# A hybrid decoder trunk step: tokens in two halves, or in five groups with two head pairs in flight

## The chip, the cores and the metric

The kernel runs on one core of one Trainium2 chip. The metric is the device time of one execution in microseconds (us), lower is better. The engines are TensorE (PE; its weight loads are shown apart as PEld), VectorE (DVE), ScalarE (ACT), GpSimd (POOL) and SyncE (SP, which only issues transfers here). Each takes its instructions in the order in which the compiled program has them. The framework in which the kernel is written chooses that order when the program is built, from a model of the durations, with the program text as priority; nothing is reordered between engines while it runs, so a wait for a late result holds up everything behind it on the same engine.

## The reference, cut to what matters

```python
D_MODEL = 1024; SEQ = 2048; DEC_BATCH = 8; DEC_SEQ = 8      # 2048 prompt tokens, 64 sample tokens
CONV_W = RWKV_W = 512; HEAD_DIM = 64; N_HEADS_RWKV = 8
IN_COLS = 4*512 + 4*512 + 64 + 64                            # 4224 = 33 tiles of 128 columns
...
xn = rms_norm(x, norm_g)
p = xn @ w_in                                                # 1024 -> 4224
u = cg * h; z = causal 3-tap conv over u; y_conv = bg * z * silu(gc)
pr = pr + mu_shift * (pr_prev - pr)                          # token shift: r, k, v, wl, al, gr
decay = exp(-DECAY_SCALE * sigmoid(w0 + tanh(wl) @ w_dec2)); a = sigmoid(a0 + al @ w_a2)
kk = normalised k * k_k
S_t = S_{t-1} diag(w_t) + (S_{t-1} (-kk_t)) (kk_t*a_t)^T + v_t k_t^T ;  o_t = S_t r_t     # per head, 64 x 64
y_rwkv = (group_norm(o) + bonus) * silu(gr)
x + concat[y_conv, y_rwkv] @ w_out, then a final rms_norm
```

Everything is float32. The prompt starts from a zero state, each of the 8 samples of 8 tokens from its own state.

## The kernel before, in words

**Layout.** Features lie on the 128 partitions and tokens along the free axis. Each large product is written as three: operands are split into a high part (rounded to the engine's faster float32 form) and a low remainder, and `project` (L305) adds high x high, high x low and low x high: 24 products for one 128-column tile of weights and one block of tokens, into one PSUM bank `pj` (two of them).

**Tokens.** The prompt is cut into two halves of 1024 (`half_blocks`, L79), each into blocks of 256, 384 and 384 tokens; the 64 sample tokens ride with the first block of the first half (330 columns with the shifted predecessors). `xprep` (L209) normalises, transposes and splits the tokens of a whole half.

**Weights.** `load_w` (L290) loads a 512 KB tile of `w_in` in the first half, splits it on ACT and POOL, and stores both parts (1 MB) to DRAM; in the second half both parts are loaded by POOL's DMA queue, into two buffers each.

**Stages.** The main loop (L923) takes 8 steps, one for each half and pair of heads. A step has: `rwkv_pair` (L423), four weight tiles (k, r, v, gate) over three blocks, each block followed by the decays, the mask products `amat` (L534; PSUM tile `ax`, 128 x 128 of scores for each 64-token chunk and head), and the rest; `inverse` (L633), which inverts the triangular 64 x 64 matrix of each chunk: the 32 x 32 diagonal blocks go through DRAM (`dn`, then `na`), are solved by a substitution of 31 steps with two DVE instructions each (`subst`, L607; tiles `sub` and `xi`), return through DRAM (`dx`, then `AB`), and two rounds of small products fill in the off-diagonal block; `wkv` (L719), the chain over the 16 chunks of 64 tokens, one after the other; and `conv_group` (L325), four weight tiles of the convolution branch, which depend on nothing of the chain. Because the order is chosen by modelled time, the conv products are placed into the gaps of `inverse` and `wkv`.

**One chunk** (`chunk`, L722) works on two heads of 64 channels, in quarters of the PE array: `ca<-sv,L` and `oo<-sv,L` (state and values against both score matrices), `cb<-sv,bt`; a DVE copy `xs`; `ca<-xs,AB`; a DVE scaling `u`; `cb<-u,bt` and `oo<-u,AB`; and one DVE instruction for each head that writes the next state. These are 12 products, or 24 instructions, since one in plain float32 is two passes.

**Output.** After all 8 steps `out_weights` (L876) loads and splits `w_out`, and `out_tile` (L890) runs 17 times over 128 tokens: 48 products of 512 columns with tokens on the partitions, residual, norm and store.

Of the kernel before, what the change touches and what calls it, by code (L numbers as in the profile page):

```python
# [17 lines left out]
D = 1024  # L18
# [8 lines left out]
HALF = SEQ // 2  # L27
CONV_COLS = 4 * CW
DS = math.exp(-0.5)
# [3 lines left out]
TW = 386  # L33

C_ID, C_BONES, C_HSEL = 0, 128, 256
NCONST = 258
C_MASK, C_SMASK, C_SCM, C_SCS, C_BM = 0, 128, 256, 640, 704
NMASK = 712

P_MU, P_KK, P_KA, P_RK, P_LG, P_LB, P_W0, P_A0, P_CW = 0, 17, 21, 25, 29, 33, 37, 41, 45  # L40
NPRM = 57


def constants():
# [7 lines left out]
    c[:, C_ID:C_ID + 128] = p[:, None] == p[None, :]  # L52
    strict = (s[:, None] < t[None, :])
    incl = (s[:, None] <= t[None, :])
    same = (s[:, None] // 8 == t[None, :] // 8)
    m[:, C_MASK:C_MASK + 64] = strict
    m[:, C_MASK + 64:C_MASK + 128] = incl
    m[:, C_SMASK:C_SMASK + 64] = strict & same
    m[:, C_SMASK + 64:C_SMASK + 128] = incl & same
    c[:, C_BONES:C_BONES + 128] = (p[:, None] // 64) == (p[None, :] // 64)  # L60
    c[:, C_HSEL] = p < 64
    c[:, C_HSEL + 1] = p >= 64
    m[:, C_SCM:C_SCM + 384] = (np.arange(384) % 64 != 0)[None, :]
# [5 lines left out]
class Blk:  # L69
    def __init__(self, i, cols, c0, np_, p0, samp, base):  # L70
        self.i, self.cols, self.c0, self.np, self.p0, self.samp = i, cols, c0, np_, p0, samp
        self.o = base + p0
        self.t0 = 0 if samp else self.o
        self.nt = np_ + (SAMP if samp else 0)
        self.ch0 = p0 // CH
        self.nch = np_ // CH


def half_blocks(hf):  # L79
    if hf == 0:  # L80
        return [Blk(0, 330, 74, 256, 0, True, SAMP), Blk(1, 384, 0, 384, 256, False, SAMP),
                Blk(2, 384, 0, 384, 640, False, SAMP)]
    return [Blk(0, 256, 0, 256, 0, False, 0), Blk(1, 384, 0, 384, 256, False, 0),
            Blk(2, 384, 0, 384, 640, False, 0)]
# [3 lines left out]
def trunk_kernel(ctx, tc, I, O):  # L88
# [4 lines left out]
    for nm in ("const", "xn", "w", "half", "pair", "tmp", "small", "ch"):  # L93
        pools[nm] = ctx.enter_context(tc.tile_pool(name=nm, bufs=1))
# [4 lines left out]
    def T(pool, shape, tag, bufs=1, dt=F32):  # L99
        cnt[0] += 1  # L100
        return pools[pool].tile(shape, dt, tag=tag, bufs=bufs, name=f"{tag}_{cnt[0]}")

# [10 lines left out]
    def tmp():  # L113
        return T("tmp", [128, TW], "t", 7)

# [11 lines left out]

    def mm(out, lhsT, rhs, start=True, stop=True):
        pe.matmul(out, lhsT=lhsT, rhs=rhs, start=start, stop=stop)  # L129

    yd = [[dram.tile([D, bl.nt], F32, name=f"yd{hf}{bl.i}") for bl in half_blocks(hf)] for hf in range(2)]
# [7 lines left out]
    bones = cst[:, C_BONES:C_BONES + 128]  # L139
    hsel = cst[:, C_HSEL:C_HSEL + 2]  # L140
    msk = T("const", [128, NMASK], "msk", 1, BF16)
    bmask = msk[:, C_BM:C_BM + 8]

    def rowtile():
        return T("half", [128, HALF + SAMP], "la0", 1)[:, :D]


# [40 lines left out]
    def rsqrt(x, n, rows=128, tag="x"):  # L188

        w = {"g": 6, "n": 3, "x": 1}[tag]  # L190
        nb = 2
        y = T("small", [128, w], "nwy" + tag, nb)[:rows, :n]
        a = T("small", [128, w], "nwa" + tag, nb)[:rows, :n]
# [10 lines left out]

# [4 lines left out]
    def xprep(hf):  # L209
        grow = rowtile()  # L210
        if hf == 1:
            act.dma_start(out=grow, in_=I["norm_g"].partition_broadcast(128).rearrange("p a d -> p (a d)"))
        if hf == 0:
            act.dma_start(out=cst[:, 0:128], in_=I["consts"][:, 0:128])
        xh, xl = [], []
        stage = [0]

        def staging():
            stage[0] += 1
# [6 lines left out]
        for bl in half_blocks(hf):  # L226
# [11 lines left out]
            if bl.samp:  # L238
                pool.memset(ss, 1.0)
# [779 lines left out]
```

## Time and profile before

| | |
|---|---|
| median of 3 runs | 1636.35 us (1623.49 to 1639.68) |
| the profiled execution: its time / its span in the trace | 1631.2 us / 1629.4 us |
| mean granted TensorE clock | 0.966 of 2.4 GHz |
| instructions | 29,336, of them 11,088 matmuls |
| PE / DVE / ACT / POOL busy | 93% / 62% / 38% / 18% |
| bytes moved | 151.9 MB |

The profile gives each instruction's start and length. Matmuls are pipelined, so their lengths overlap: what a product costs is the distance from its start to the next one's. "pj<-xh,wh" is an instruction that writes tile pj from the tiles xh and wh.

### The profile page before, as it was taken

Reading aid. Unit: us, or ns where it says so; the run is one execution under the profiler, and the core shown is the slowest. Engines: PE = TensorE matmul, PEld = TensorE weight load, DVE = VectorE, ACT = ScalarE, POOL = GpSimd, SP = SyncE. Lnnn points to the kernel's source line nnn. Section 1 sums busy time; section 2 is a strip of 40 time slices with the busy share of each in tenths; the row PEclk is TensorE's granted clock in tenths of the full one; section 3 lists DMA queues with packets and bytes.
Section 4 is the critical chain, followed back from the end, with each engine's and each line's share of the span. In section 5 each row is a group of like instructions: output and inputs, shape, how many; then the busy total and the mean of one; then the engine's idle time right before and its main releaser. Section 6 shows DMA issues by size and latency. Waiting matters only on the chain.

```text
span 1629.4 us, 29336 instructions
## 1 busy us (share of the span) xinstructions
PE 1519.4 (93%) x11088; PEld 1267.0 (78%) x11088; DVE 1006.0 (62%) x3101; ACT 615.4 (38%) x1591; POOL 288.6 (18%) x395
## 2 busy tenths in 40 slices
PE   4989999989999999969999999989999999899997
PEld 4979778887788777866789778977897788667885
DVE  7377558664686458775576358735863587466544
ACT  6343346224542344435442245124513443343221
POOL 3233202320142103311013002200220023000000
PEclk9989999799999998999999899999998999899999
DMA  6323421241133312451213212321232135523441
GB/s 226 122 80 103 130 68 64 90 132 61 48 127 115 100 49 86 146 140 34 62 61 94 82 35 63 97 79 35 62 108 68 35 88 165 149 69 127 139 139 52
DMA packets 121967, 151.90 MB, mean 93 GB/s; under 512 B 62617, under 2 KB 86681, under 8 KB 121826
## 3 DMA queue, kind: packets, MB, share of 16 engines
q1 hardware_dynamic: 107024, 104.53, 20.9%
q0 software_dynamic: 9536, 34.64, 6.6%
q10 hardware_dynamic: 5266, 10.86, 1.8%
q8 instruction: 88, 1.44, 0.4%
q14 instruction: 53, 0.43, 0.1%
HBM read 92.60 MB, written 57.35 MB: 92 GB/s over the span
## 4 chain that ended last, share of the span: by engine, by line
PE 64%; DVE 23%; DMA 5%; issue 3%; ACT 3%; SPq 1%; POOL 0%; ACTq 0%; DVEq 0%; POOLq 0%
PE pj L129 42%; PE ca L129 5%; PE ax L129 5%; DVE xi L123 4%; DVE sub L123 4%; PE cb L129 4%; DVE hp L123 3%; PE oo L129 2%; PE cx L129 2%; DVE t L120 1%; DMA dx<-xi 1%; DVE bk L123 1%; PE cx L696 1%; DMA AB<-dx 1%; DVE hp L120 1%
## 5 line engine op out<-in xcount | busy, mean ns | idle before, releaser
L129 PE MATMUL pj<-xh,wh 128*128 128x384 f32 (+3 forms) x1856 | 655.7, 354 | 15.3 <-DVE hp L123 12.5
L129 PE MATMUL pj<-xl,wh 128*128 128x384 f32 (+3 forms) x1856 | 650.4, 350 | 3.7 <-DVE xl L207 1.9
L129 PE MATMUL pj<-xh,wl 128*128 128x384 f32 (+3 forms) x1856 | 651.3, 351 | 0.1
L129 PEld LDWEIGHTS pj<-xh,wh 128*128 128x128 f32 x1856 | 356.0, 192 | 48.7 <-DVE hp L123 11.9
L129 PEld LDWEIGHTS pj<-xl,wh 128*128 128x128 f32 x1856 | 356.4, 192 | 33.3 <-DVE xl L207 4.5
L129 PEld LDWEIGHTS pj<-xh,wl 128*128 128x128 f32 x1856 | 354.9, 191 | 27.4 <-issue 2.8
L117 ACT ACTIVATE tS<-sv,wc 64x64 f32<-64x64 f32 x256 | 88.1, 344 | 121.3 <-DVE sv L120 95.8
L207 POOL TENSOR_TENSOR wl<-wr,wh 128x512 fp32r<-128x512 f32 x66 | 86.9, 1329 | 191.3 <-ACT wh L117 188.2
L120 DVE SCALAR_TENSOR_TENSOR sv<-cb,wc,tS 64x64 f32<-64x64 f32 x240 | 67.9, 283 | 68.8 <-PE cb L129 62.4
L129 PE MATMUL ax<-L,bk 64*128 64x128 f32 x528 | 83.6, 309 | 22.1 <-DVE bk L123 14.9
L129 PEld LDWEIGHTS ax<-L,bk 64*128 64x128 f32 x528 | 69.7, 206 | 39.4 <-issue 20.2
L117 ACT ACTIVATE t<-pj,prm 128x384 f32<-128x384 f32 (+3 forms) x170 | 68.6, 433 | 68.3 <-PE pj L129 64.8
L524 POOL TENSOR_TENSOR bk<-t,t 64x384 f32<-64x384 f32 (+2 forms) x56 | 57.0, 1019 | 164.4 <-ACT t L496 75.1
L123 DVE TENSOR_TENSOR sub<-xi,na 128x126 f32<-128x126 f32 (+22 forms) x248 | 76.2, 307 | 16.1 <-DMA na<-dn 8.9
L744 DVE TENSOR_SCALAR u<-ca,Q 128x64 f32<-128x64 f32 x128 | 36.2, 283 | 80.4 <-PE ca L129 80.2
L123 DVE TENSOR_TENSOR xi<-xi,sub 128x126 f32<-128x126 f32 (+22 forms) x248 | 79.5, 321 | 7.3
L117 ACT ACTIVATE wh<-wr 128x512 fp32r<-128x512 f32 x66 | 40.5, 626 | 90.4 <-PE pj L129 79.2
L129 PEld LDWEIGHTS ca<-sv,L 128*64 128x64 f32 x528 | 43.0, 134 | 37.9 <-DVE sv L120 13.8
L734 DVE COPY xs<-ca 128x64 f32<-128x64 f32 x128 | 28.7, 224 | 66.2 <-PE ca L129 55.4
L129 PE MATMUL ca<-sv,L 128*64 128x64 f32 x528 | 67.4, 245 | 0.1
L294 POOL DMA_DIRECT2D wh<-wsp x33 | 18.7, 566 | 252.6 <-PE pj L129 177.4
L123 DVE TENSOR_TENSOR hp<-hp,pj 128x384 f32<-128x384 f32 (+2 forms) x56 | 25.6, 464 | 55.2 <-PE pj L129 55.0
(203 smaller groups left out, 2055.0 us busy)
## 6 DMA issues: line engine op xcount, KB each, us to landing
wr<-in_w_in SPq DMA_DIRECT2D x66, 256.0 KB, 3.7
wsp<-wh SPq DMA_DIRECT2D x33, 512.0 KB, 2.8
wsp<-wl SPq DMA_DIRECT2D x33, 512.0 KB, 4.0
wh<-wsp POOLq DMA_DIRECT2D x33, 512.0 KB, 3.6
wl<-wsp POOLq DMA_DIRECT2D x33, 512.0 KB, 4.7
hp<-in_x_prompt SPq DMA_DIRECT2D x29, 512.0 KB, 3.7
la<-yd SPq DMA_DIRECT2D x16, 512.0 KB, 4.1
out_y_p<-hp ACTq DMA_DIRECT2D x16, 512.0 KB, 2.6
```

What stands on the lines that cost most here:

```text
L117: act.activation(out=out, in_=in_, func=AF.Copy, scale=scale, bias=bias)
L120: eng.scalar_tensor_tensor(out=out, in0=in0, scalar=scalar, in1=in1, op0=op0, op1=op1)
L123: dve.tensor_tensor(out=out, in0=in0, in1=in1, op=op)
L129: pe.matmul(out, lhsT=lhsT, rhs=rhs, start=start, stop=stop)
L207: eng.tensor_tensor(out=lo, in0=src, in1=hi.bitcast(F32), op=ALU.subtract)
L294: pool.dma_start(out=wh, in_=wsp[col, 0])
L524: pool.tensor_tensor(out=S.bk[bl.i][hs, chs, h, :], in0=ta[hs, a:a + n].rearrange("p (c j) -> p c j", j=64), in1=wi[hs, a:a + n].rearrange ...
L696: pe.transpose(out=pb[:, i, :], in_=S.bk[bi][:, ca + i].rearrange("p a t -> p (a t)"), identity=ident)
L734: dve.tensor_copy(out=xs_, in_=px)
L744: dve.tensor_scalar(out=u, in0=pu, scalar1=S.Q[:, q:q + 1], scalar2=None, op0=ALU.mult)
```

## The change

- **Five groups of tokens** take the place of the two halves: one of 256 prompt tokens with the 64 samples, then four of 448 (7 chunks). A weight tile now serves one group, so each group goes through all 33 input tiles. The first group splits the weights and stores them; the four others load 1 MB for each tile. The buffers of high and low weights go from two to three.
- **Two pairs live.** A step is now a group and a pair of heads: 20 steps. The masks, score matrices, values and gates of a pair exist twice (`LP`, `GP`, `ABP`). `inverse` and `wkv` are generators, and the main loop advances them a bit (three substitution portions, or one chunk) after each weight tile of the same step's convolution and of the next step.
- **Full 128 x 128 recurrence.** `chunk` multiplies by whole matrices: one product for each head gives both the read of the state and its output part, one gives `u` for both heads, and one for each head gives the state's update and the rest of the output: 5 products, 10 instructions. The output of four chunks stays in PSUM and is added after the fourth.
- **Solving four columns of blocks at once**: `subst` works on 8 columns at a time in place of 16, on blocks repeated four times over the partitions.
- **Output feature-major.** `out_group` treats `w_out` as 8 more weight tiles against the group's outputs. The products of group q stand in the program beside the convolution tiles of group q+1; the last group's stand alone at the end. Sums of squares over features are taken by PE; the un-normalised output goes to DRAM and comes back.
- `xprep` of the next group stands beside the conv tiles too, one token tile at a time.

The core of the diff:

```diff
-HALF = SEQ // 2
+NG = 5
+G0, GN = 256, 448
+NC = 7
...
+    def load_w(i, first):
+        wh = T("w", [128, KT, 128], "wh", 3, F32R)
+        wl = T("w", [128, KT, 128], "wl", 3, F32R)
+        if not first:
+            pool.dma_start(out=wh, in_=wsp[i][0])
+            pool.dma_start(out=wl, in_=wsp[i][1])
+            return wh, wl
...
+    def chunk(S, c, wc, sv, i, nxt, pc, sample=None):
+        for h, hs in heads():
+            mm(pc[h][:, 0, i, :], S.L[h][:, c, :], sv[:, i, h, :])
+        xd = XD[i % 2]
+        if sample is None:
+            tS = T("ch", [128, 64], "tS", 2)
+            for h, hs in heads():
+                copy(tS[hs], sv[hs, i, h, :], scale=S.wc[hs, wc:wc + 1])
+            dve.tensor_copy(out=xd[0:64, 0:64], in_=pc[0][0:64, 0, i, :])
+            copy(xd[64:128, 64:128], pc[1][64:128, 0, i, :])
...
+        pu = pc[2][:, i, :]
+        mm(pu, S.AB[:, c:c + 2, :].rearrange("p c t -> p (c t)"), xd)
+        dve.tensor_scalar(out=sv[0:64, i, 0, :], in0=pu[0:64, 0:64], scalar1=S.Q[0:64, c:c + 1], scalar2=None,
+                          op0=ALU.mult)
+        copy(sv[64:128, i, 1, :], pu[0:64, 64:128], scale=S.Q[64:128, c:c + 1])
+        for h, hs in heads():
+            mm(pc[h][:, 1, i, :], S.Gm[h][:, c, :], sv[:, i, h, :])
+        if sample is None:
+            for h, hs in heads():
+                stt(nxt(h)[hs], pc[h][hs, 1, i, :], S.wc[hs, wc:wc + 1], tS[hs], ALU.mult, ALU.add)
...
+    def out_group(G):
+        nt = G.nt
+        yh, yl = (t[:, :, 0:nt] for t in XB[G.q % 2])
+        for k in range(KT):
+            raw = T("tmp", [128, GN], "oy", 2)[:, :nt]
+            sync.dma_start(out=raw, in_=yd[G.q][k * 128:(k + 1) * 128, :])
+            copy(yh[:, k, :], raw, scale=0.5)
+            stt(yl[:, k, :], raw, 0.5, yh[:, k, :].bitcast(F32), ALU.mult, ALU.subtract)
...
+            ps = product(NIN + m, G.q == 0, yh, yl)
+            tt(xt, ps, xt, ALU.add)
...
+            sync.dma_start(out=xo[G.q][f, :], in_=xt)
+            yield
...
+    for G in groups:
+        la = lora_tiles(G)
+        for p in range(NPAIR):
+            while len(tasks) > 1:
+                drain(tasks.pop(0))
+            S = Pair(G, p)
+            for _ in rwkv_pair(S, la):
+                advance()
+            tasks.append(chain(S))
+            if p == 1 and G.q:
+                out = out_group(groups[G.q - 1])
+            if p == (1 if G.q == 0 else 3) and G.q < NG - 1:
+                pre = xprep(groups[G.q + 1])
+            for _ in conv_group(G, p):
+                advance()
+                next(pre, None)
+                for _ in range(1 if p < 3 else 4):
+                    next(out, None)
+    for t in tasks:
+        drain(t)
+    drain(out)
+    drain(out_group(groups[-1]))
```

## Rows read from the trace of the kernel before

**Rows 1.** The page, busy time of each engine: us, share of the span, instructions.

```profile
PE 1519.4 (93%) x11088; PEld 1267.0 (78%) x11088; DVE 1006.0 (62%) x3101; ACT 615.4 (38%) x1591; POOL 288.6 (18%) x395
```

**Rows 2.** Windows: stretch, length, busy by engine (instructions), PE clock, DMA share, GB/s.

```profile
0.00:45.00 45.00, 22.08 (x119) 18.63 (x120) 32.73 (x71) 28.72 (x53) 13.88 (x30) 0.99 0.61 205
...
670.00:740.00 70.00, 55.83 (x430) 50.46 (x429) 49.16 (x146) 28.37 (x59) 17.32 (x19) 0.94 0.45 129
...
990.00:1030.00 40.00, 37.74 (x237) 33.63 (x236) 33.27 (x71) 15.38 (x34) 10.77 (x17) 1.00 0.31 91
1030.00:1080.00 50.00, 44.83 (x354) 42.78 (x352) 26.03 (x83) 8.94 (x25) 10.28 (x16) 0.93 0.35 98
1080.00:1150.00 70.00, 68.99 (x645) 53.20 (x644) 38.48 (x164) 33.16 (x99) 4.49 (x9) 1.00 0.11 37
```

**Rows 3.** Timeline of PE: first and last of 48 products of 384 columns.

```profile
1040.26 0.34 PE L129 MATMUL pj<-xh,wh 128*128 128x384 f32 x1
...
1048.41 0.33 PE L129 MATMUL pj<-xh,wl 128*128 128x384 f32 x1
```

**Rows 4.** Timeline of PE: first and last of 27 products of 512 columns.

```profile
1499.81 0.39 PE L129 MATMUL pj<-xh,wl 128*128 128x512 f32 x1
...
1505.79 0.40 PE L129 MATMUL pj<-xl,wh 128*128 128x512 f32 x1
```

**Rows 5.** Timeline of PE over one chunk of the chain: start, length, instruction, count.

```profile
1111.91 0.34 PE L129 MATMUL pj<-xh,wl 128*128 128x384 f32 x1
1112.18 0.33 PE L129 MATMUL ca<-sv,L 128*64 128x64 f32 x2
...
1112.99 0.44 PE L708 MATMUL cx<-cst,v 128*128 128x128 f32 x2
1113.36 0.33 PE L129 MATMUL ca<-xs,AB 64*64 64x64 f32 x4
1113.62 0.44 PE L129 MATMUL pj<-xh,wh 128*128 128x384 f32 x1
1113.90 0.34 PE L129 MATMUL pj<-xl,wh 128*128 128x384 f32 x1
...
1114.34 0.33 PE L129 MATMUL cb<-u,bt 64*64 64x64 f32 x4
...
1114.72 0.44 PE L129 MATMUL pj<-xh,wh 128*128 128x384 f32 x1
...
1115.27 0.27 PE L129 MATMUL ca<-sv,L 128*64 128x64 f32 x1
```

**Rows 6.** Timeline of PE: two runs of mask products, 12 and 6 instructions.

```profile
1005.60 1.57 PE L129 MATMUL ax<-L,bk 64*128 64x128 f32 x12 [0.43 <-DVE bk L123]
...
1008.09 0.90 PE L129 MATMUL ax<-L,bk 64*128 64x128 f32 x6
```

**Rows 7.** The page, groups of the substitution: busy us, mean ns, then idle before them.

```profile
L123 DVE TENSOR_TENSOR sub<-xi,na 128x126 f32<-128x126 f32 (+22 forms) x248 | 76.2, 307 | 16.1 <-DMA na<-dn 8.9
...
L123 DVE TENSOR_TENSOR xi<-xi,sub 128x126 f32<-128x126 f32 (+22 forms) x248 | 79.5, 321 | 7.3
```

**Rows 8.** Groups by form, VectorE: the substitution's instructions of 70 elements.

```profile
L123 DVE TENSOR_TENSOR sub<-xi,na 128x70 f32<-128x70 f32 x8 | 1.8, 230 | 0.1
```

**Rows 9.** The chain that ended last, the inverse of one pair: start, us, what.

```profile
1186.70 4.27 DMA dn<-AB
...
1191.71 3.72 DMA na<-dn
...
1217.23 3.85 DMA dx<-xi
...
1222.01 3.68 DMA AB<-dx
```

**Rows 10.** The page, DMA issues: count, KB each, median us to landing.

```profile
wh<-wsp POOLq DMA_DIRECT2D x33, 512.0 KB, 3.6
wl<-wsp POOLq DMA_DIRECT2D x33, 512.0 KB, 4.7
```

More of the change, by code (lines that the diff above doesn't have):

```diff
@@ L92, in trunk_kernel @@
     pools = {}
-    for nm in ("const", "xn", "w", "half", "pair", "tmp", "small", "ch"):
+    for nm in ("const", "xn", "w", "pair", "tmp", "small", "ch"):
         pools[nm] = ctx.enter_context(tc.tile_pool(name=nm, bufs=1))
@@ L101, in T, with DT @@
         return pools[pool].tile(shape, dt, tag=tag, bufs=bufs, name=f"{tag}_{cnt[0]}")
+    def DT(shape, tag, bufs=1):
+        cnt[0] += 1
+        return dram.tile(shape, F32, tag=tag, bufs=bufs, name=f"{tag}_{cnt[0]}")
     def PS(shape, tag, bufs):
@@ new lines, in trunk_kernel, with xprep @@
+    XB = [[T("xn", [128, KT, GN], f"x{n}{i}", 1, F32R) for n in "hl"] for i in range(2)]
+    def xprep(G):
+        h, l = (t[:, :, 0:G.cols] for t in XB[G.q % 2])
+        rows = []
+        if G.samp:
+            act.dma_start(out=ident, in_=I["consts"][:, 0:128])
+            sr = T("small", [128, 144], "sub", 1)[:, :KT * NB].rearrange("p (k b) -> p k b", k=KT)
+            rows.append((I["x_sample"], SAMP, None))
+        for i in range(0, G.np, 128):
+            n = min(128, G.np - i)
+            rows.append((I["x_prompt"][G.tok + i:G.tok + i + n, :], n, G.c0 + i))
+        for i, (src, n, o) in enumerate(rows):
+            xt = T("tmp", [128, D], "xr", 2)[:n]
+            sync.dma_start(out=xt, in_=src)
+            if G.samp and i == 0:
@@ L305, in project @@
[L305 to L316 removed]
+                continue
@@ new lines, in product, with project @@
+    def product(i, first, xh, xl):
+        wh, wl = load_w(i, first)
+        ps = PS([128, xh.shape[-1]], "pj", 2)
+        for k in range(KT):
+            mm(ps, wh[:, k, :], xh[:, k, :], start=(k == 0), stop=False)
+            mm(ps, wh[:, k, :], xl[:, k, :], start=False, stop=False)
+            mm(ps, wl[:, k, :], xh[:, k, :], start=False, stop=(k == KT - 1))
+        return ps
+    def project(G, col):
+        return product(col // 128, G.q == 0, *(t[:, :, 0:G.cols] for t in XB[G.q % 2]))
@@ new lines, in shifted @@
+    def shifted(G, i, ps, out):
+        mb = tmp()
+        if not G.samp:
+            copy(mb[:, 0:1], carry[:, i:i + 1])
+        n = G.cols
+        copy(mb[:, 1:1 + n], ps, scale=pcol(P_MU, i))
+        copy(carry[:, i:i + 1], mb[:, n:n + 1])
+        om = omm[:, i:i + 1]
+        if G.samp:
+            stt(s8(out), s9(ps)[:, :, 1:9], om, s9(mb[:, 1:])[:, :, 0:8], ALU.mult, ALU.add)
+        stt(out[:, G.o:G.nt], ps[:, G.c0:n], om, mb[:, G.c0:n], ALU.mult, ALU.add)
+    LP = [[T("pair", [128, NC, 128], f"L{h}{i}") for h in range(2)] for i in range(2)]
@@ new lines, in trunk_kernel, with drain, chain, advance @@
+    tasks = []
+    def drain(task):
+        for _ in task:
+            pass
+    def chain(S):
+        for i, _ in enumerate(inverse(S)):
+            if i % 3 == 2:
+                yield
+        yield
+        yield from wkv(S)
+    def advance():
+        for t in list(tasks):
+            if next(t, 0) == 0:
+                tasks.remove(t)
+    clear_blocks()
+    drain(xprep(groups[0]))
+    derive()
+    load_masks()
+    out = iter(())
+    pre = iter(())
+    for G in groups:
[16 more added lines that the diff above has]
+                    next(out, None)
```

1079 lines of the change are left out of this document (450 added, 629 removed).

## The prediction

> **What bounds the kernel now.** I read the page's busy times first, then the windows of one steady pair, then PE's timeline inside one chunk. PE is busy for 1519.4 of 1629.4 us [rows 1], but that hides two things. Of the 110 us without any product, 22.9 lie before 45 us, while the first half's tokens are prepared, 14.2 at the second half's preparation, and 8.5 (2.3 + 5.2 + 1.0) in the 160 us of one steady pair, 990 to 1150 us [rows 2]. And in `wkv` PE looks busy (68.99 of 70 us) where it is not fed well: so I price products by the distance from start to start.
>
> The large products cost (1048.41 - 1040.26)/47 = 0.1734 us at 384 columns [rows 3] and (1505.79 - 1499.81)/26 = 0.2300 us at 512 [rows 4], that is 0.000442 us a column more or less: 0.1168 at 256, 0.1451 at 320, 0.1495 at 330, 0.2017 at 448. Before: 33 tiles x 24 = 792 products on each block, 792 x (0.1495 + 0.1168 + 4 x 0.1734) = 760 us, and 17 x 48 of the output, 188 us: 948 us of stream.
>
> One chunk of the chain takes three visits of PE [rows 5]: 1112.18 to 1112.99, 1113.36 to 1113.62 and 1114.34 to 1114.72, 1.45 us. Each visit also makes the stream product before it 0.10 us longer (1111.91 to 1112.18 is 0.27 in place of 0.173) and the one after it 0.11 us (1113.62 to 1113.90 is 0.28). With 3 x 0.2 a chunk costs 2.05 us, and 33 chunks x 4 pairs = 132 of them 271 us.
>
> That leaves 1629.4 - 948 - 271 - 22.9 - 14.2 = 373 us. The remaining 11,088 - 5,568 - 3,168 = 2,352 matmul instructions are mask products, transposes and the inverses' quarter-size products. A mask instruction costs (1.57 - 0.90)/6 = 0.112 us [rows 6]; at that price for all, they are 263 us, and 110 us are waits inside the pairs. (8 x 8.5 = 68 us of waits can be seen as idle, so 110 is not far off; it can't exceed 373 - 59, with the 528 mask products alone.) So PE's stream is the largest part, and what can be won are the waits and the price of a chunk.
>
> **The change part by part**, against the profiled execution's 1631.2 us (1.8 us lie outside the span).
>
> *Stream, -8 us.* After: 792 x (0.1495 + 4 x 0.2017) = 757 us, and output 8 tiles x 24 x (0.1451 + 4 x 0.2017) = 183 us: 940 for 948. Moving the output beside the next group removes none of it; it only gives the chain more to hide behind.
>
> *Chunk, -44 us.* Ten instructions with 128 columns of stationary operand take the place of 24 small ones. No row has a 128x128 float32 product with 64 columns; the nearest is the mask product, also 128 stationary columns, 0.112 us. 10 x 0.112 + 3 visits x 0.2 = 1.72 us, for 132 chunks 227 in place of 271. Bounds: the small products of the first visit are 0.81/12 = 0.068 apart [rows 5], which would give 1.28 us a chunk (-102 us); two full 128x128 products took 0.37 us (1112.99 to 1113.36), 0.185 each, which would give 2.45 us (+53 us). I take the mask product, nearest in shape and part of a run.
>
> Here the Trainium skill speaks against the change. "TensorE: Matmul & The Clock Gate" (section on LDWEIGHTS) says that a weight load takes its columns / 1.2 ns whatever its rows, and its Part 3 that small products on different row groups run at once. As an estimate from that page, 12 pairs of 64-column loads would cost 12 x 0.053 = 0.64 us a chunk before and ten 128-column loads 1.07 us after, +57 us in all. The trace agrees on the full load (0.112 us a piece), and not on the small ones, whose visits take 1.45 us. It is a rival below.
>
> *Start, -10 us.* Only three token tiles stand ahead of the first stream product in place of nine. The first two loads and the norm still take until about 28 us of the 45, but the first group then needs weights at once. Bounds -17 to 0.
>
> *Second preparation of tokens, -14 us.* The 14.2 us of idle go: preparation now stands tile by tile beside conv products. Bounds -14 to 0.
>
> *First group's weights, +15 us.* A tile's load, split and store (1.5 MB) had 24 x (0.1495 + 2 x 0.1734) = 11.9 us of PE work to hide behind; now it has 3.6, and a pair of the first group has about 30 us of stream and 20 of other work for 8.25 tiles. At 205 GB/s, the most that rows 2 show, a tile takes 7.3 us, 33 of them 241 us against 4 x 50 of PE: +41. At the full share of the DMA engines (205/0.61 = 336 GB/s) it is 148 us and hidden: 0. POOL's and ACT's splits stay the same in number. I take a third, since 205 GB/s was reached at a share of only 0.61.
>
> *Norm of the output, +5 us*, about 40 small instructions on PE at 0.112; the stores and loads of the un-normalised output lie beside other work. Bounds 0 to +10.
>
> *The end, +55 us.* Before, the last pair's chain ran beside its conv tiles and the first output tiles. Now the last group's output waits for the last chain, and only that pair's four conv tiles (4 x 24 x 0.2017 = 19 us) can cover it. The chain alone: the four transfers 4.27 + 3.72 + 3.85 + 3.68 = 15.5 us [rows 9]; 62 substitution instructions at 0.23 [rows 8], 14 us; seven chunks at 3.09 us (1112.18 to 1115.27, rows 5), 22 us; and by estimate 12 us for the products that complete the inverse, the group norm, and the way of its output through DRAM: 64 us, 45 of them bare. The last norm adds 10. Bounds +10 (if the order puts conv tiles late and the chain early) to +90.
>
> *Waits inside the pairs, -55 us.* Now an independent pair, the output tiles and the next preparation stand beside each chain, and each chain may take some twelve tiles' time. Against that: the inverse's trip through DRAM and its in-order waits on PE now come 20 times, not 8. If all are covered, -110; if each wait stays as it is and comes 20 times, 110 x 20/8, +165. I take half of the waits, because the inverse's share of them (5.2 of 8.5 us of idle) arises where PE stands at a product that needs the returned blocks, and the program now puts a whole weight tile between the return and those products. SP's queue, which carries the inverse's 16 transfers a pair in order, now also carries the output's 24 loads and 8 stores a group, each waiting for its own data; and POOL's queue holds a pair's weight loads, which wait for a free buffer, ahead of POOL's share of the mask work. What these cost is inside the bounds of this term.
>
> *VectorE* gets more: the substitutions cost 76.2 + 79.5 = 155.7 us for 8 inverses [rows 7]; now 20 x 62 = 1,240 instructions of some 50 elements on the mean. A 70-element one takes 0.230 us [rows 8]; at 0.21 that is 260 us, +105. Sums of output parts, norms tile by tile and fewer, longer instructions elsewhere add some 35: 1006 becomes about 1146 us. That is 73% of the forecast; a steady stretch holds 83% (33.27 of 40 us, rows 2). I price it at 0 in the sum, covered by PE's stream, and as a rival below.
>
> Sum: 1631 - 8 - 44 - 10 - 14 + 15 + 5 + 55 - 55 = **1575 us** on the scale of the profiled execution. The median of the runs lies 5 us above that execution: **1580 us**.
>
> **The rivals.**
> - *Full cover, 1490 us.* All waits inside the pairs go (a further -55) and half of the bare chain at the end is covered (-35). For it: PE idles only 1.0 us in the 70 us of `wkv`, so the order does fill gaps when it has material. Against it: one core's order is fixed by modelled times.
> - *No cover gained, 1635 us.* The order before already put conv tiles into `inverse` and `wkv`; what it waited for were results later than modelled, and those come as late now. The 55 us are not won.
> - *VectorE's queue becomes the pace, 1715 us: slower.* The chain's 62 + 28 short instructions per pair stand in one queue with projections' evacuations of 0.5 to 1 us; each step of the chain waits behind one, and PE behind the step. It decides from the point where VectorE can't hold 1146/1636 = 70% on the mean; before it held 62%. At 67% the time is 1146/0.67 = 1710. For it: no stretch of `inverse` or `wkv` in rows 2 goes above 55%. Against it: 83% in 990 to 1030.
> - *The recurrence loses, 1675 us.* A full product costs 0.185 us, not 0.112: 97 us more than in the sum. In a sentence of its own: the skill's two rules above would give 1580 + 44 + 57 = 1681.
> - *Weights five times over, 1690 us.* Groups two to five load 1 MB a tile; if the two halves land one after the other, 3.6 + 4.7 = 8.3 us [rows 10], 41 x 4 tiles take 1361 us, with 220 for the first group and 110 for both ends. Against it: three buffers, and a DMA share of 0.11 to 0.35 over the steady pair [rows 2].
>
> **How the numbers follow.** Forecast 0.40 (its own range 1520 to 1620), full cover 0.15, no cover gained 0.17, VectorE 0.14, weights 0.08, recurrence 0.06. About 1% (16 us) is what a measurement of this kernel tells from no change, so 1620 to 1652 is "same": faster 0.55, same 0.17, slower 0.28. The terms with wide bounds (waits -110 to +165, chunk -102 to +53, end +10 to +90) rarely go one way together; the range 1480 to 1700 takes in full cover and most of the slower rivals and leaves about 2 in 10 out.
>
> **What would show it.** Right: stream products of 448 columns 0.20 us apart; a chunk with three visits of PE and about 1.7 us of its time; idle of PE at the end of 40 to 60 us, before 8 output tiles in one piece; VectorE at 70 to 75%. Wrong: full products more than 0.15 us apart; idle of PE spread over each pair above 5 us; PE waiting for wh; VectorE under 68% with PE idle behind `sub`, `xi` or the state's update.

## The result, and the profile after

The changed kernel takes 1862.26 us (median of 4 runs, 1859.78 to 1864.57), beside 1638.01 us for the kernel before (4 runs, 1623.49 to 1639.88): a ratio of 1.139, 95% interval 1.132 to 1.146. It is 14% slower. The forecast was 1580 us and its range ended at 1700.

The page of the kernel after, busy times, to be laid beside [rows 1], and the granted clock in 40 slices:

```profile
span 1861.9 us, 26776 instructions
...
PE 1500.5 (81%) x8724; PEld 1276.5 (69%) x8724; DVE 1154.2 (62%) x3823; ACT 730.7 (39%) x1981; POOL 510.8 (27%) x750
...
PEclk9778787889999998999999699999987999999767
```

PE's busy time fell by only 18.9 us and its idle time rose from 110.0 to 361.4 us, by 251.4. The difference, 232.5 us, is the whole loss of span. VectorE's busy time came to 1154 us (forecast 1146). The mean granted clock went from 0.966 to 0.892.

The clock hides a part of what happened to PE. By the clock records of the two traces, PE was busy for 245 us at the 1.2 GHz level (granted clock 0.50) after the change, and for 97 us before. A product of 448 columns starts 0.373 us after the one ahead of it at that level and 0.203 us at the full clock (medians over the trace), so as an estimate the 148 us more cost some 67 us. At equal clocks PE's busy time would have fallen by some 86 us, not 19.

Windows over the five groups, to be laid beside [rows 2]: stretch, length, busy by engine (instructions), PE clock, DMA share, GB/s.

```profile
0.00:400.00 400.00, 272.02 (x1529) 230.67 (x1530) 253.20 (x833) 160.03 (x433) 133.20 (x179) 0.81 0.54 180
400.00:700.00 300.00, 263.40 (x1583) 227.87 (x1581) 209.46 (x694) 126.00 (x340) 93.61 (x132) 0.95 0.62 189
700.00:1050.00 350.00, 300.30 (x1765) 255.51 (x1765) 222.49 (x747) 142.12 (x385) 90.96 (x142) 0.92 0.59 173
1050.00:1400.00 350.00, 299.93 (x1765) 254.78 (x1765) 221.06 (x744) 142.23 (x386) 91.03 (x142) 0.92 0.58 172
1400.00:1690.00 290.00, 260.11 (x1552) 221.00 (x1553) 180.10 (x560) 116.81 (x320) 78.16 (x121) 0.94 0.57 166
1690.00:1862.00 172.00, 104.72 (x535) 86.66 (x533) 67.86 (x246) 43.54 (x120) 23.84 (x36) 0.78 0.47 146
```

And the kernel before, in three stretches of the same kind:

```profile
0.00:400.00 400.00, 358.61 (x2562) 309.91 (x2563) 246.91 (x689) 161.09 (x404) 100.37 (x135) 0.96 0.34 110
400.00:1457.00 1057.00, 997.56 (x7750) 830.35 (x7748) 666.61 (x2105) 414.23 (x1093) 188.22 (x260) 0.96 0.28 84
1457.00:1629.40 172.40, 163.27 (x782) 126.72 (x778) 92.50 (x311) 40.09 (x94) 0.00 (x0) 0.99 0.35 114
```

Read as length minus PE busy: 128 us of idle in the first 400 us (41 before), 166 in the middle (59 before), 67 in the last 172 us (9 before). All three places lose. VectorE is nowhere full: 60 to 70%, and 39% in the last 172 us.

What PE waits for, its largest waits (us in total, times, longest):

```profile
PE cx L782 <- ACT c L775: 88.3, 48, 9.9
PE ax L265 <- DVE xr L128: 57.2, 11, 11.8
PE pj L143 <- ACT wh L125: 26.2, 14, 4.8
...
PE ax L143 <- ACT wdh L125: 15.3, 2, 8.4
...
PE pj L143 <- POOL wl L221: 13.9, 19, 1.8
```

They are the transposes of the group norm (L782) and of the token preparation (L265), and the first group's weights (wh and wl, and wdh, the high part of the weights of the decays). The same list of the kernel before has no wait above 14.9 us, and no wait for wh or wl.

The stream and one chunk on PE, 1003 to 1019 us, to be laid beside [rows 3 to 5]:

```profile
1003.34 0.36 PE L143 MATMUL pj<-xl,wh 128*128 128x448 f32 x1
...
1005.97 0.36 PE L143 MATMUL pj<-xh,wl 128*128 128x448 f32 x1
...
1014.56 0.55 PE L143 MATMUL ch<-sv,L 128*128 128x64 f32 x4
1014.92 0.45 PE L143 MATMUL pj<-xh,wh 128*128 128x448 f32 x1
1015.21 0.37 PE L143 MATMUL pj<-xl,wh 128*128 128x448 f32 x1
...
1016.22 0.38 PE L143 MATMUL cu<-xd,AB 128*128 128x128 f32 x2
1016.36 0.45 PE L143 MATMUL pj<-xh,wh 128*128 128x448 f32 x1
...
1017.06 0.35 PE L143 MATMUL ch<-sv,G 128*128 128x64 f32 x2
1017.22 0.45 PE L143 MATMUL pj<-xh,wh 128*128 128x448 f32 x1
...
1017.91 0.33 PE L143 MATMUL ch<-sv,G 128*128 128x64 f32 x2
1018.05 0.45 PE L143 MATMUL pj<-xh,wh 128*128 128x448 f32 x1
1018.34 0.36 PE L143 MATMUL pj<-xl,wh 128*128 128x448 f32 x1
```

The stream's pitch is 2.63/13 = 0.202 us. A chunk takes 0.36 + 0.14 + 0.16 + 0.14 = 0.80 us of its own, and the stream product behind each of its four visits takes 0.29 in place of 0.20: 1.16 us in all, where 1.72 was forecast and 2.05 was the price before.

And one typical stop, 941 to 958 us, in three timelines (SP, VectorE, PE):

```profile
941.36 3.37 SPq L609 DMA_DIRECT2D dx<-xi  x4
...
948.73 1.80 SPq L613 DMA_DIRECT2D AB<-dx  x4
```

```profile
953.85 0.41 DVE L617 STREAM_TRANSPOSE na<-AB 128x224 f32<-128x224 f32 x1 [5.73 <-DMA AB<-dx]
954.18 0.12 DVE L128 SCALAR_TENSOR_TENSOR nwyg<-nwag,nwyg 128x7 f32<-128x7 f32 x1
...
954.94 0.17 DVE L128 SCALAR_TENSOR_TENSOR gm<-gm,nwyg 128x7 f32<-128x7 f32 x1
```

```profile
951.77 0.37 PE L143 MATMUL pj<-xh,wl 128*128 128x448 f32 x1
955.97 0.48 PE L782 MATMUL cx<-cst,c 128*128 128x128 f32 x1 [3.83 <-ACT c L775]
...
957.72 0.71 PE L143 MATMUL pj<-xh,wh 128*128 128x448 f32 x1
958.23 0.57 PE L143 MATMUL pj<-xl,wh 128*128 128x448 f32 x1
958.61 0.57 PE L143 MATMUL pj<-xh,wl 128*128 128x448 f32 x1
```

The window behind the stop, as in the windows above:

```profile
955.60:961.00 5.40, 4.66 (x13) 3.58 (x14) 2.81 (x6) 2.40 (x7) 0.00 (x0) 0.50 0.56 204
```

The younger pair's inverted blocks go out from 941.36 and are back at 953.85. VectorE stands 5.73 us at the instruction that needs them (L617). Behind it in VectorE's queue is the rest of the older pair's group norm (nwyg, gm); behind that ScalarE's scaling; behind that PE's transposes, and behind those the stream products, which need none of it. So PE stands 3.83 us. Then it pays once more: the granted clock behind the stop is 0.50, and the next products are 0.51 and 0.38 apart in place of 0.20. PE's list names ScalarE; the late one is a transfer of another pair.

### The profile page after: what moved, and what is told of

Read it like the earlier page. It is cut to its first block, busy times and chain, and to the rows that moved or that the text cites. A ratio compares the mean times of both kernels' runs of the same rounds, so it can differ in the third digit from the quotient of the medians.

```text
span 1861.9 us, 26776 instructions
## 1 busy us (share of the span) xinstructions
PE 1500.5 (81%) x8724; PEld 1276.5 (69%) x8724; DVE 1154.2 (62%) x3823; ACT 730.7 (39%) x1981; POOL 510.8 (27%) x750
## 4 chain that ended last, share of the span: by engine, by line
PE 39%; DVE 21%; DMA 11%; ACT 6%; issue 3%; SPq 2%; POOL 0%; DVEq 0%; POOLq 0%; ACTq 0%
PE pj L143 25%; PE ax L143 5%; DVE sub L131 5%; DVE xi L131 4%; PE ch L143 4%; DMA oy<-xo 2%; PE cu L143 2%; DMA dx<-xi 2%; DVE bk L131 2%; DMA AB<-dx 1%; ACT sv L125 1%; SPq L609 1%; DMA oy<-yd 1%; PE cx L143 1%; DMA out_y_p<-oy 1%
## 5 line engine op out<-in xcount | busy, mean ns | idle before, releaser
L143 PE MATMUL pj<-xh,wh 128*128 128x448 f32 (+2 forms) x1640 | 641.7, 392 | 41.1 <-ACT wh L125 26.2
L143 PE MATMUL pj<-xh,wl 128*128 128x448 f32 (+2 forms) x1640 | 631.8, 385 | 16.9 <-POOL wl L221 13.9
L143 PE MATMUL pj<-xl,wh 128*128 128x448 f32 (+2 forms) x1640 | 628.4, 383 | 0.0
L131 DVE TENSOR_TENSOR sub<-xi,na 128x60 f32<-128x60 f32 (+24 forms) x620 | 167.7, 270 | 21.4 <-DMA na<-dn 7.0
L131 DVE TENSOR_TENSOR xi<-xi,sub 128x60 f32<-128x60 f32 (+24 forms) x620 | 158.9, 256 | 14.3
L143 PEld LDWEIGHTS ch<-sv,G 128*128 128x128 f32 x528 | 92.2, 200 | 26.1 <-DVE sv L672 8.5
L143 PE MATMUL ch<-sv,G 128*128 128x64 f32 x528 | 98.4, 271 | 5.2 <-DVE sv L672 4.2
L782 PE MATMUL cx<-cst,c 128*128 128x128 f32 x72 | 28.2, 413 | 88.3 <-ACT c L775 88.3
L143 PEld LDWEIGHTS ch<-sv,L 128*128 128x128 f32 x528 | 80.5, 197 | 20.7 <-ACT sv L125 7.1
L277 POOL DMA_DIRECT2D wl<-wsp x164 | 89.9, 548 | 9.6 <-PE pj L143 6.3
L143 PE MATMUL ch<-sv,L 128*128 128x64 f32 x528 | 83.3, 274 | 7.2 <-ACT sv L125 4.5
```

Of the source, the lines that this page charges most:

```text
L131: dve.tensor_tensor(out=out, in0=in0, in1=in1, op=op)
L277: pool.dma_start(out=wl, in_=wsp[i][1])
L782: pe.transpose(out=pt[0:w, i, :], in_=ob[:, e + 2 * i:e + 2 * i + w // 64, :].rearrange("p c v -> p (c v)"), identity=ident)
```

## The experiments

Each kernel is the changed one with one edit, unless its name begins with b or h (the kernel before with one edit). The kernel before took 1626.8 to 1637.3 us beside them, so differences under about 1% between single runs are not read. The period of a group is the time from one group's `la`, the first tiles that a group computes, to the next one's: 331.9, 348.4, 350.6 and 348.7 us in the changed kernel.

**Four suspects, one at a time.**

*The last norm.* `out_group` stores the un-normalised tiles as the output; the second pass (loads, scaling, stores) is left out. The sums of squares on PE stay.

```diff
-            sync.dma_start(out=xo[G.q][f, :], in_=xt)
+            sync.dma_start(out=O["y_p"][f, G.tok:G.tok + G.np], in_=xt[:, G.o:nt])
```

The four were predicted together, from one set of theories: A the last norm, B the first group's weights, C VectorE's pace, D the five loads of the weights.

> The changed kernel without the second pass of its output: the un-normalised sums go straight to the results, the stores to DRAM, the 40 loads, the 40 last VectorE instructions and the 45 last stores fall away; so the final norm is left out. Theory A (the second pass stalls VectorE's and SP's queues: each load waits for a store to free one of two buffers, and what stands behind waits too, 25 to 29 us of idle PE in each change of groups and some 30 us at the end): 1862 goes to 1720 to 1760 us, and the dips of PE at 1000 to 1050 and 1350 to 1400 us go. Theory B (first group's weights): 1840 or more, only the end gets shorter. Theory C (VectorE's pace): 40 x 0.7 = 28 us of VectorE less, about 1820. Theory D (weights loaded five times): 1845, 18 MB of 323 less.

1822.4 us, -40. From the start of the last stream product to the end it takes 14 us in place of 31; the three middle periods are 2 to 10 us shorter, the first is 2 longer. A is a small part. (The time is also the one that theory C named; e3 is the test of C.)

*The split.* Both parts of a weight tile are loaded from the input in every group; splitting and storing are left out, also for the 8 tiles of `w_out`.

```diff
-        if not first:
...
+        pool.dma_start(out=wh, in_=I["w_io"][i])
+        pool.dma_start(out=wl, in_=I["w_io"][i])
```


> The changed kernel with each weight tile's two parts loaded by POOL's queue straight from the input in every group, the first one too: no raw load, no split on ACT and POOL, no store (the low parts are then the full weights; the splitting is left out). Bytes of groups two to five are the same. Theory B (the first group waits for load, split and store of 1.5 MB a tile through two half-tile buffers and SP's order): the first group ends near 240 us in place of about 400, in all 1700 to 1740 us. Theories A, C and D: 1840 to 1862 us.

1757.1 us, -105, a little above theory B's range. The first period falls from 331.9 to 240.5 us; the others nearly stay (344, 348, 351). The largest piece, and 91 us of it in one place. PE's idle time falls by 68 us and its busy time, at a mean clock of 0.910, by 39.

*Half the substitution*, with `by` = 2:
```diff
-        for s in range(n - 1):
+        for s in range(0, n - 1, by):
```


> The changed kernel with every second step of the 31 substitution steps left out: 15 x 2 x 20 = 600 VectorE instructions of 0.26 us fewer, 157 us of 1154; so the inverse is not the true one. Theory C (VectorE can't hold more than the 62% it shows): 1862 x (1154 - 157)/1154 = 1610 us. Theories A, B and D: 1820 to 1862 us, by what the shorter chain gives at the end (8 us) and in its waits.

1803.1 us, -59, outside both ranges, with 120 us less of VectorE's busy time (1034.2). If its work set the pace, all 120 would have gone.

*Half the weights' traffic.*
```diff
-            pool.dma_start(out=wl, in_=wsp[i][1])
-            return wh, wl
+            return wh, wh
```


> The changed kernel loading only the high part of each weight tile in groups two to five and using it twice (the low part's product is then a wrong one): 82 MB of 323 and 164 POOL transfers fewer. Theory D (five passes over the weights set the pace of groups two to five): 1700 us or less, each group 40 us shorter. Theories A, B and C: 1835 to 1865 us.

1818.9 us, -43, for 86 MB less: below the range of the other theories, and far above D's 1700, so not the pace either.

**Four edits that leave nothing out.** e5, and the same for `wl`:

```diff
-        sync.dma_start(out=wsp[i][0], in_=wh.bitcast(F32))
+        pool.dma_start(out=wsp[i][0], in_=wh.bitcast(F32))
```


> The first group's weights: the stores of the split parts are issued from GpSimd's queue, right behind its own split, and not from SP's, where each holds up the next load until ACT and GpSimd are done. In the first 400 us PE stands 55 us behind wh, wl and wdh, and runs at a granted clock of 0.67 to 0.86. If SP's order is what delays the loads, 1760 to 1810 us, and SP no longer waits for wh ahead of a load. If the pace is set by the splits themselves on ACT and GpSimd or by the traffic, 1840 to 1865.

1819.4 us, -43: between the two ranges. In the first 400 us of the changed kernel SP stood at these stores, with the next loads behind them:

```profile
SPq L283 <- ACT wh L125: 69.8, 19, 10.7
SPq L284 <- POOL wl L221: 25.4, 20, 2.5
SPq L281 <- POOL wl L221: 16.1, 13, 3.5
```

After the edit it stands at the loads themselves, for a free half-tile buffer, which GpSimd's subtraction gives back:

```profile
SPq L281 <- POOL wl L221: 116.1, 45, 10.3
```

So the order of the stores is 43 of the 105 us. PE's waits for wh, wl and wdh, 55 us before the edit, are 20 us after it. What the other 62 us of e2 are is not shown. The two half-tile buffers are one candidate. Another is on VectorE, whose same 3,823 instructions took 1088.1 us in e2, 66 less than in the changed kernel. While GpSimd subtracts, an instruction of the substitution can take 1.2 us in place of 0.22 (VectorE, then GpSimd):

```profile
84.50 0.22 DVE L131 TENSOR_TENSOR sub<-xi,na 128x60 f32<-128x60 f32 x1
...
85.56 1.22 DVE L131 TENSOR_TENSOR sub<-xi,na 128x72 f32<-128x72 f32 x1
```

```profile
85.39 1.29 POOL L221 TENSOR_TENSOR wl<-wr,wh 128x512 fp32r<-128x512 f32 x1 [3.55 <-ACT wh L125]
```

Against the median of their form elsewhere in the trace, VectorE's instructions beside such a subtraction take some 52 us more in the changed kernel, and some 35 in the kernel before.

e6, the last norm tile by tile, its loads one ahead:

```diff
-            if m % 4 == 3:
-                yield
+            yield
...
-                for _ in range(1 if p < 3 else 4):
+                for _ in range(1 if p < 3 else 2):
```


> The second pass over the output (last norm) one tile at a time, each load issued one tile ahead, over the four tiles of the last pair and the first of the next group, in place of eight tiles at once. If that burst holds VectorE and SP and so makes the token preparation late (PE stands 41 us behind xr between 400 and 1690 us), 1815 to 1840 us. Leaving the pass out altogether gave 1822, which is the floor for this. If the preparation is late by itself, 1850 to 1865.

1861.0 us: nothing. The waits at L265 only change their name (32.0 behind xr, 33.0 behind sub).

e7, in `gn_out` (the pause before it in `wkv` goes):

```diff
             act.activation(out=ob[:, i, :], in_=ob[:, i, :], func=AF.Identity, scale=r[:, i:i + 1],
                            bias=m[:, i:i + 1])
+        yield
         yo = T("ch", [128, 8 * 64], "c2", 4)[:, :n * 64]
```


> Group norm: its statistics and scaling one weight tile ahead of its transposes (the pause that stood before the statistics now stands behind them). PE stands 88 us at these transposes for ACT's scaled c, 56 of them between 400 and 1690 us. If it is the order alone (PE comes to the transposes before the scaling can be done), 1780 to 1815 us, with the wait at that line under 25 us. If VectorE is behind as a whole, the wait moves to the next product that needs it: 1850 to 1865.

1865.7 us: nothing; the wait at that line is 73.6 us, not under 25. In a middle group the compiled program puts the transposes of two pairs 40 stream products behind the last chunk, with and without the edit: text order is a priority only, and VectorE is as late as before.

e8, in `xprep`, the norm of tile i + 1 ahead of the transposes of tile i:

```diff
+        nx = norm(0)
+        if not G.samp:
+            yield
...
+            xt = nx
+            if i + 1 < len(rows) and not G.samp:
+                nx = norm(i + 1)
```


> Token preparation: the norm of each 128 tokens one weight tile ahead of its transposes. PE stands 57 us at these transposes for the normed rows xr, 41 of them between 400 and 1690 us. If it is the order alone, 1805 to 1830 us with the wait at that line under 20 us. If VectorE is behind as a whole at the change of groups, 1850 to 1865.

1826.6 us, -36. The wait behind xr falls to 37.6 us, not under 20; the middle periods are 333 to 340 us in place of 348 to 351.

**The return, the stream, and the recurrence alone.** e9, in `inverse`:

```diff
-            sync.dma_start(out=dx[:, :, :, :, q, :].rearrange("h b c s t -> (h b c) s t"), in_=x[q * 32:q * 32 + U])
...
-                sync.dma_start(out=AB[r:r + 32, e:e + nch, b * 32:b * 32 + 32],
-                               in_=dx[h, b].rearrange("c s q t -> (s q) c t"))
```


> The changed kernel without the return of the inverted diagonal blocks through DRAM (the four stores dx and four loads of AB of each pair are left out; the substitution is still done). VectorE stands 42.7 us in order at the first instruction that needs the returned block, with the other pair's group norm and evacuations queued behind it, and PE stands 88 us at the group norm's transposes. If that trip is what makes results late all along a pair, 1770 to 1820 us, and the period of a middle group (349 us from one group's first instruction to the next one's) falls by 10 to 20 us. If it is only one late result among many, 1835 to 1860.

1773.1 us, -89, and the wait at the transposes falls from 88.3 to 51.1 us. The periods become 320, 339, 325 and 330. For 20 pairs that is 4.4 us a trip. PE's idle time falls by 63 us and its busy time, at a mean clock of 0.906, by 28.

e10, and b1 the same in the kernel before:

```diff
-            mm(ps, wh[:, k, :], xl[:, k, :], start=False, stop=False)
```


> The changed kernel without the high x low product of every weight tile: 16 products in place of 24, a third of PE's stream, 313 us at the pitch of before the change's forecast. If PE's stream still sets the pace and the waits are only added to it, 1550 to 1600 us. If the chains of dependent steps of two pairs and the in-order waits behind them set the pace, most of the 313 us come back as idle of PE: 1690 to 1780.

1665.0 us, -197 of 313, at a mean clock of 0.813: below the range of the second theory, above that of the first.

> The kernel before with the same left out (the high x low product of every weight tile, and in the output the product with the low part of w_out): 316 us of PE's stream. If PE's stream sets its pace, 1320 to 1370 us. If it is as much bound by its chains as the changed kernel, above 1450.

1612.6 us, only 15 less. Its page:

```profile
PE 1384.5 (86%) x9232; PEld 1113.3 (69%) x9232; DVE 987.8 (61%) x3101; ACT 618.0 (38%) x1591; POOL 286.3 (18%) x395
...
PEclk9978776696568955696966885887578857899999
```

and two windows of its recurrence:

```profile
975.00:1000.00 25.00, 21.81 (x169) 15.62 (x168) 13.75 (x57) 10.52 (x30) 1.30 (x2) 0.50 0.02 6
...
1150.00:1175.00 25.00, 22.47 (x157) 16.13 (x158) 13.87 (x53) 10.40 (x32) 1.47 (x2) 0.50 0.02 7
```

With all the products the recurrence ran at a granted clock of 1.00 [rows 2, 1080 to 1150 us]; without a third of them these stretches ran at 0.50, the 1.2 GHz level. The clock's mean fell from 0.966 to 0.781. PE's busy time fell by only 135 of the 316 us, so 181 us came back as longer busy time on what was left, and idle of PE rose by 116, from 110 to 226. So this run doesn't separate chain from stream. It shows that products taken out of the old order are not won; whether a chain would have set the pace at the full clock stays open.

h1 puts the full 128x128 recurrence of the change into the kernel before (five products; matrices built for four chunks at a time, in the place of two temporary buffers) and leaves the rest.

```diff
-            for h, hs in heads():
-                mm(px[hs], L[h][:, c, 0:64], sv[:, i, h, :])
-            for h, hs in heads():
-                mm(po[hs], L[h][:, c, 64:128], sv[:, i, h, :], start=True, stop=False)
+            for h, hs in heads():
+                mm(pc[h][:, 0, i, :], S.L[h][bi][:, c, :], sv[:, i, h, :])
...
+            mm(pu, S.AB[bi][:, c, :], xd)
...
+                mm(pc[h][:, 1, i, :], bt[h][:, i, :], sv[:, i, h, :])
```

> The kernel before with one part of the change alone: the recurrence in full 128x128 products (5 products, 10 instructions a chunk), everything else as before (two temporary buffers given up for the larger matrices). In the changed kernel a chunk takes about 1.2 us of PE's stream, against 2.05 before. If the price on PE decides, 132 x 0.85 us are won: 1510 to 1540 us. By my prediction's term (-44 us) 1590. If the chain's steps over ScalarE and VectorE set the pace in that stage, 1620 to 1650.

1620.0 us, -8, too little to read from one run. So it was run again:

> The kernel before with the full 128x128 recurrence alone, timed again in five rounds, since one run gave 1620 us beside 1627.6. If the chunk's price on PE is worth anything in the old order, 0.4 to 0.8% faster; if that was chance, within 0.3% of the kernel before.

1623.3 us beside 1634.5, ratio 0.9939, interval 0.991 to 0.9968: 0.6% faster than the kernel before, about 10 us, a small difference but clear of the noise.

```profile
PE 1487.6 (92%) x9272; PEld 1303.4 (81%) x9272; DVE 1031.4 (64%) x3189; ACT 711.0 (44%) x1967; POOL 317.8 (20%) x488
```

PE's busy time falls by 32 us, its idle time rises by 20, and the mean clock is 0.934 in place of 0.966. Read by starts, a chunk costs some 1.2 us of PE here too, 0.85 less than before; it is worth 10/132 = 0.08 us. The chunks do not come closer together either: inside a run of chunks (distances under 12 us) the median from one to the next is 3.95 us, before it was 3.72.

**Do the pieces add up?** f1 has the edits of e2 and e9, f2 those of e1 and e3 as well, and b2 is the edit of e9 in the kernel before (its own form of the same stores and loads).

> The changed kernel with the two largest pieces left out together: the split and stores of the first group's weights (both parts loaded ready in every group) and the return of the inverted blocks through DRAM. Alone they gave -105 and -89 us. If they are separate causes in separate places, 1660 to 1680 us. If both only hide the same waits, or the next late result takes their place, 1710 to 1755.

1667.5 us: they are separate.

> The same, and also every second step of the substitution and the second pass over the output left out (alone -59 and -40 us). If these four pieces are what the changed schedule pays for, 1862 - 105 - 89 - 59 - 40 = 1569 us, near my forecast. If new late results take their place, 1620 to 1680: then the cause is the order with nothing to fill a wait, not these pieces.

1569.9 us: the four pieces add up to within 1 us. That it is near the forecast proves nothing of the design, since it leaves out work that the kernel before does as well.

> The kernel before without the return of the inverted blocks through DRAM (stores dx and loads of AB left out, the substitution still done). The changed kernel lost 89 us by 20 returns, 4.4 us each. At the same price each, 8 returns cost 36 us here: 1590 to 1600. If the old order covered the trip with its convolution tiles, 1610 to 1632.

1634.2 us: in the old order the trip costs nothing, though VectorE stands at the returned blocks there too:

```profile
DVE na L673 <- DMA AB<-dx: 13.1, 6, 4.4
```

That makes the 89 us a loss of the change.

e11 joins e5, e8 and, for the last group, `out_group` without the trip of its tiles through DRAM (they stay in the buffers of `LP`):

```diff
-            sync.dma_start(out=xo[G.q][f, :], in_=xt)
+            if not last:
+                sync.dma_start(out=xo[G.q][f, :], in_=xt)
```

> The changed kernel with nothing left out and three edits: the stores of the first group's weights on GpSimd's queue (-43 alone), the norm of 128 tokens one weight tile ahead of its transposes (-35 alone), and the last group's un-normalised output held in the score matrices' buffers in place of a trip through DRAM (the 31 us after the last product fall to about 15). If they add up, 1765 to 1780 us. If they overlap, 1790 to 1815.

1761.4 us (ratio 1.078, 1.070 to 1.086): -101, so they add up (the third was not run alone). From the last stream product to the end it is 19 us.

**In order, or too long a chain?** e13 is e11 with the first use of the returned blocks tied to a later result:

```diff
         yield
+        yield
+        copy(na[:, 0, 0:1], latest[0][:, 0:1])
         t1, ys = na[:, 0:nch, :], na[:, NC:NC + nch, :]
...
-            if i % 3 == 2:
+            if i in pauses:
```

`latest` is the newest weight tile's result, and `pauses` is (3, 8, 9), in the first group (5, 9, 10), where it was each third step.

> The kernel of the three edits (1761 us) with nothing left out and the first use of the returned blocks made later: two weight tiles after the loads are issued in place of one, held there by a one-column copy from the newest weight tile's result; the substitution is done in two portions in place of three to make room. If the 89 us of the return come from VectorE standing in order at the returned block with other work queued behind it, the wait for AB on VectorE falls from some 40 us to under 15 and the time to 1690 to 1730 us. If they come from the length of the chain (the trip must be over before the recurrence can start), 1750 to 1790.

1715.4 us (4 runs, 1706.5 to 1725.0; ratio 1.048, 1.043 to 1.054), 46 less than e11. VectorE's wait for the trip falls from 41.0 us to 9.6, and PE's wait at the group norm from 65.6 to 34.7 (e11, then e13):

```profile
DVE na L630 <- DMA AB<-dx: 41.0, 11, 6.4
PE cx L795 <- ACT c L788: 65.6, 36, 11.1
```

```profile
DVE na L635 <- DMA AB<-dx: 9.6, 3, 4.2
PE cx L800 <- ACT c L793: 34.7, 19, 11.4
```

The trip is still made. From a pair's first store `dx` it takes 13.4 us on the mean to VectorE's first use of the blocks (12.0 in e11), and 21.6 us to the first product of the recurrence (23.5 in e11). So the result lies in the range of the first theory and the wait went as it says, but the chain did not stay as long as it was: up to the recurrence it got 1.9 us a pair shorter. The edit changes two things, the place of the first use and the portions of the substitution, and no run has one alone: 46 of the 89 us come back by them together, and that all 46 are VectorE standing in order is not shown.

## Why the prediction was wrong, step by step

Two terms of the sum carry most of the miss: the waits inside the pairs (-55) and the first group's weights (+15). Here are the parts of the sum beside the three stretches of the two traces (the stretches don't hold quite the same work; the measured numbers for PE's products and for the clock are the estimate above):

| part | forecast, us | measured, us |
|---|---|---|
| PE idle, first 400 us: start -10, first group's weights +15 | +5 | +87 |
| PE idle, middle: waits -55, second preparation -14 | -69 | +107 |
| PE idle, last 172 us: the end | +55 | +58 |
| PE's products: stream -8, chunk -44, norm +5 | -47 | -86 at equal clocks |
| the lower clock | no term | +67 |
| sum | -56 | +233 |

Two of the prediction's signs of being wrong are there: PE waits for wh (26.2 us), and idle of PE is above 5 us a pair (50 us in 350 for four pairs).

- **Waits inside the pairs, -55: wrong in sign.** Between the first 400 us and the last 172, idle rose from 59 to 166 us. The reason given, "the program now puts a whole weight tile between the return and those products", looked at PE. The wait moved to VectorE, which stands at L617 with the other pair's work behind it. 20 returns at 4.4 us are 89 us (e9) where 8 cost nothing (b2). The upper bound of the term (+165, each wait 20 times in place of 8) was the right thought, and half of the waits was the wrong choice. The 110 us of waits were also a remainder: idle outside the two preparations was 73 us, and the slow clock, 97 us of busy time before, lies in the rest.
- **First group's weights, +15: mis-sized.** 105 us (e2), beyond its upper bound of +41, though e2 was not run in the old order. Both ends counted traffic, 7.3 us a tile. For 43 us (e5) it was the order that held: load, split on ScalarE, subtraction on GpSimd, store, and on SP's queue the next load behind that store. The rest is open. With 11.9 us of PE's work a tile the old order covered it, as far as PE's waits show: its list has none for wh or wl.
- **What bounds the kernel now: a ledger in PE's time at the full clock.** "PE's stream is the largest part, and what can be won are the waits and the price of a chunk." It is the largest part of PE's time, but savings in it were not won one for one: a third of the stream out of the old kernel gave 15 us of 316 (b1), the cheaper chunk about 10 of the 112 that 132 x 0.85 us make (h2). Part came back as idle and part as a lower clock, for which the ledger has no term. In f2, at a mean clock of 0.957, the same 8,724 matmul instructions are busy for 1416.7 us, 84 less than in the changed kernel at 0.892.
- **Second preparation, -14, and start, -10: wrong in sign.** The preparation beside the conv tiles costs 57 us of waits at L265; e8 took 36 us of time back with 20 us of these waits. The first stream product comes at 34.6 us; before it came at 20.3.
- **Chunk, -44: the price was forecast too high, and so was its worth.** A chunk costs PE 1.16 us in place of the forecast 1.72, and in the old order that saving is worth 10 us, not 44 (h2). The rival "the recurrence loses" falls with it: the first visit's four instructions take 0.36 us, 0.09 each, not 0.185. The estimate from the Trainium skill ("TensorE: Matmul & The Clock Gate", section on LDWEIGHTS) was 1.07 us for the ten loads and 0.64 us for the 24 small products. The trace has 0.80 us for the ten, 1.16 with the stream's share; for the small ones the old trace shows 1.45 without it.
- **Stream, -8: right** at the full clock (pitch 0.2023, forecast 0.2017). **The end, +55: right**: 67 us of idle in the last 172, 9 before. **Norm of the output, +5: mis-sized**, 40 us for the second pass with its trip through DRAM (e1).
- **VectorE** has the work that was forecast in total, by luck: the substitution's 1,240 instructions took 327 us where 260 was forecast, and the rest 58 less than forecast. The rival "VectorE's queue becomes the pace" named the sign and the place, but its mechanism was short instructions behind evacuations. By its own rule the 62% that VectorE holds would give 1146/0.62 = 1848 us, near the result; yet VectorE is not full, it is stopped. **Weights five times over** falls: half the traffic is worth 43 us (e4).

Removal gives 105 us for the first group's weights, 89 for the return, 59 for half the substitution and 40 for the second pass. Only the return was also taken out of the kernel before, so only its 89 us are shown to be a loss of the change. The kernel before splits its weights, substitutes and normalises too, and what that costs there was not tested. The edits that leave nothing out (e11, e13) took 147 us back. After e13, 81 us (1715.4 to 1634.5) are left. PE's idle time there is 91 us in the first 350, 110 in the middle 1210 and 53 in the last 163 (busy 259.4, 1099.9 and 110.2); the bare chain at the end is part of it, and no run took it away.

## What to carry to other kernels

When two independent chains share engines that take instructions in order, one chain's late transfer stops the other chain and the filling work behind it. Before adding a second chain, list for every engine what stands behind each instruction that waits for a transfer, and tie that instruction to a later result. In e7 moving another instruction's text alone changed nothing, as the order is chosen by modelled time; e13, with a data dependency, did. And before pricing a saving in an engine's time, ask what comes in its place: in b1 and h2 most of it came back, as idle and as a lower granted clock.

## What the runs showed of the hardware that was not expected

Leaving out work slowed what was left. With a third of the products gone the old kernel's recurrence ran at a granted clock of 0.50 for whole stretches, with PE still 87 to 90% busy, and 316 us of products were worth 15. The changed kernel at 0.813 kept 197 of 313. Some of VectorE's small instructions took 1.2 us in place of 0.22 while GpSimd subtracted. And a trip of a pair's 32 x 32 blocks through DRAM (four stores, four loads) took 12.5 us, 3.4 of which were the issue of the four stores alone.
